# One core, hybrid decoder layer in split f32r products: h's tiles become operands of the output products in place, the last gate reads hL first, the early gate is finished at once, conv tiles are turned later

## The chip, the cores and the metric

One NeuronCore of a Trainium2 chip runs the whole kernel in one launch. The metric is the device time of one execution in microseconds (us); the kernel before took 1667.37 us as the median of three runs (1662.56 to 1667.37). The engines are TensorE (PE, its weight loads are listed apart as PEld), VectorE (DVE), ScalarE (ACT), GpSimd (POOL) and SyncE (SP), which here only issues DMAs.

## The reference

One layer of a decoder trunk over 1024 tokens of width 1024 (S = D = 1024), float32. All branches read the same normalised input, through one big projection:

```python
h = rms_norm(x, norm_g)
proj = h @ w_in                      # 9616 columns
sb_cols, ssd_cols, rw_cols, gate_cols = _split(proj, [2048, 2320, 2176, 3072])
y_sb  = stick_breaking_attention(q, k, v) * silu(sb_gate)      # 8 heads x 64
y_ssd = rms_norm(ssd_mixer(xbc, dt_raw, ...) * silu(z), ssd_norm_g)   # conv of 4 taps, 16 heads, chunks of 128
y_rw  = rwkv7_mixer(rw_cols, ...) * silu(rw_gate)              # 8 heads x 64
g_sb, g_ssd, g_rw = split(sigmoid(gate_cols))                  # 3 x 1024
merged = g_sb*(y_sb @ w_out_sb) + g_ssd*(y_ssd @ w_out_ssd) + g_rw*(y_rw @ w_out_rw)
out = rms_norm(x + merged @ w_o, final_g)
```

## The kernel before, in words

**Split products.** Every large product is made of three f32r matmuls: an operand v is kept as hi (v rounded to f32r) and lo (the rest), and hi·Hi + hi·Lo + lo·Hi go into one PSUM bank. h itself, turned so that its 1024 features lie on partitions, is kept on chip as hH and hL, each 128 x 8 x 1024 (k = 0..7 is the block of features). A weight block of 128 columns comes as `wraw` (one buffer, 512 KB from memory, L193), is cast by ACT into `whi` (L194) and subtracted by DVE into `wlo` (L195), two buffers each; the function is `wload`.

**One projection** (`proj`, L229 to L243) makes 128 columns of the big product: for each half th of the tokens (512) a PSUM bank `pj` (two of them) collects 8 x 3 matmuls of 128x512, a step being the three of one k. So a projection is 16 steps, 48 matmuls. When a half is full, `use` empties it: for the RWKV columns `shift_mix` (ACT L257, DVE L258, a one-column copy `lst` L261, and L264), for the merge gates ACT's sigmoid into `sgt` (L283) and a store to `sgd` in memory, for the conv columns ACT L736, three DVE additions L738 and three small ones L745, then ACT's Silu over the whole tile (L746).

**What sets the order.** TensorE's instructions are written in the order they run. A planner (`Driver`) makes that order: it counts a model time T.t from the matmuls issued, keeps a list `small` of chains (the mixers' small products; a chain may wait a given model time, or for a condition) and issues their next piece when it is due; else it issues one step of the projection at hand (`drv.cur`, `step_big`): first those that the stage needs (`big`), then the 24 merge gates (`spare`), which nothing needs before the output products. Projections are thus the filler between the small products. The planner's numbers fix only the order; the other engines' orders are found by the framework's scheduler from the dependencies, and each engine runs its own list in order.

**Stages.** Start: x is loaded, its rows normalised (`stat`, L297 to L301), turned and split into hH and hL (L309, L310) while two projections already run: `first` (the low-rank RWKV columns, tile `lo`) and `early`, the first merge gate. Their last four steps each alternate, then `drv.cur = first` and `early`, whose second half is still undone, goes back to the front of the gates (L345 to L349): from there it holds one `pj` bank and one `whi`/`wlo` pair until a gate is wanted as filler.
Then RWKV (`rwkv`, 4 units). Then the SSD branch: conv columns c0 to c9; the step sizes dt and the decays da by a chain of small DVE work (to L820), 16 steps of filler (L821), three small products of da with triangle matrices li, ls and on, whose exponentials EX are made on ACT (L824 to L829, all in bank `pma`, of which there are two buffers); then the chunk scan: the conv tiles are turned to token order (`to_tok`, L752) when the tile's conv is done and, for the first group, 2.5 of model time later; then 2 groups x 8 chunks, in which `first(c)` makes the masked decays Mt (L912, L918) and `second(c)` uses them. Then z's gate, a norm (L996) with stores to `yssd`, and 18 steps of filler before the attention's pools take the SSD's space.
Then attention in 4 head pairs: projections Q, K, V, gT of the pair, and 8 rows of 128 queries each (L1097 to L1133): scores, two sigmoids on ACT (be, kp), a mask on POOL, a scan on DVE (L1103), transposes and the product with v. When the projections and gates are all issued, the output products become the filler: `outs` has the RWKV output (`yr`, read back from memory, 4 blocks of k) and then the SSD output (`yssd`, 8 blocks); after the rows come the attention's output and the last product with w_o.

**The output's operands.** `ysplit` loads a block of y (`yt`, four buffers), casts it to yH (L1149, ACT) and subtracts to yL (L1150, DVE). yH and yL have pools of their own (oyA, oyB), which take the space of hH and hL after `hp_ctx.close()`; `reuse_waits="tile"` makes each new tile wait for the tiles whose space it takes. `outp` makes the products, multiplies with the stored merge gate `sg` (L1174 or the lines after it) and stores or adds up `mo`.

Of the kernel before, what the change touches and what calls it, by code (L numbers as in the profile page):

```python
# [8 lines left out]
F32 = mybir.dt.float32  # L9
F32R = mybir.dt.float32r  # L10
# [5 lines left out]
P = 128  # L16
S = 1024
D = 1024
# [120 lines left out]
def body_(tc, A, out):  # L139
# [14 lines left out]
    def pm(tag="a", hold=0.0):  # L154
        drv.bank(tag, hold)
        return psm.tile([P, HB], F32, name="pm" + tag)
# [20 lines left out]
                src = src.rearrange("o (c p) -> (o c) p", p=P)  # L177
            nc.sync.dma_start(out=prow[PO[n]:PO[n] + k, :], in_=src)

    hp_ctx = ctx.enter_context(ExitStack())  # L180
    hp_ = hp_ctx.enter_context(tc.tile_pool(name="hp_", bufs=1, side="right"))
    hH = hp_.tile([P, KT, S], F32R, name="hH")
    hL = hp_.tile([P, KT, S], F32R, name="hL")
    w_in = A["w_in"][0]
# [46 lines left out]
    def proj(c0, use):  # L231

        hi, lo = ahead.pop(c0, None) or wload(w_in[:, c0:c0 + P])
        for th in range(2):
            sl = slice(th * HB, (th + 1) * HB)
            ps = psp.tile([P, HB], F32, name="pj")
            for k in range(KT):
                T.matmul(ps, lhsT=hi[:, k, :], rhs=hH[:, k, sl], start=(k == 0), stop=False)
                T.matmul(ps, lhsT=hi[:, k, :], rhs=hL[:, k, sl], start=False, stop=False)
                T.matmul(ps, lhsT=lo[:, k, :], rhs=hH[:, k, sl], start=False, stop=(k == KT - 1))  # L240
                if k == KT - 1:
                    use(th, ps)
                yield  # L243

    loc = ctx.enter_context(ExitStack())
    lstp = loc.enter_context(tc.tile_pool(name="lstp", bufs=2, side="right"))
    lop = loc.enter_context(tc.tile_pool(name="lop", bufs=1, side="right"))
# [32 lines left out]
    def gate(b, m):  # L280
        def use(th, ps):
            o = gt.tile([P, HB], F32, name="sgt")
            ACT.activation(out=o, in_=ps, func=AF.Sigmoid)  # L283
            nc.sync.dma_start(out=sgd[b, m * P:(m + 1) * P, th * HB:(th + 1) * HB], in_=o)

        return proj(C_GATE + b * D + m * P, use)


    gates = [gate(b, m) for b in (2, 1, 0) for m in range(8)]
# [21 lines left out]

    for t in range(4):
        stat(t)
    pss = [pm("bcbca"[k]) for k in range(5)]
    for i in range(4):
        if i == 3:
# [25 lines left out]
        elif k > 3:  # L342
            next(first)
    x0c.close()
    for _ in range(4):  # L345
        next(first)
        next(early)
    drv.cur = first
    gates.insert(0, early)  # L349


    def rwkv():
# [349 lines left out]
    def ssd():  # L702
# [22 lines left out]
        cT = cc.tile([P, S], F32, name="cT")  # L725
        bt = cc.tile([P, NT, P], F32, name="bt")

        done = set()

        def conv(c, dst):  # L730
            w = lambda k: par("conv_w", k * 10 + c)
            kept = []

            def use(th, ps):
                o = dst[:, th * HB:(th + 1) * HB]
                ACT.activation(out=o, in_=ps, func=AF.Identity, scale=w(3), bias=par("conv_b", c))  # L736
                for d in range(1, 4):
                    stt(out=o[:, d:], in0=ps[:, 0:HB - d], scalar=w(3 - d), in1=o[:, d:], op0=MUL, op1=ADD)  # L738
                if th == 0:
                    lst = wk.tile([P, 3], F32, name="lst")  # L740
                    V.tensor_copy(out=lst, in_=ps[:, HB - 3:HB])
                    kept.append(lst)
                else:
                    for d in range(1, 4):
                        stt(out=o[:, 0:d], in0=kept[0][:, 3 - d:3], scalar=w(3 - d), in1=o[:, 0:d], op0=MUL, op1=ADD)  # L745
                    ACT.activation(out=dst, in_=dst, func=AF.Silu)  # L746
                    done.add("c%d" % c)

            return proj(C_XBC + c * P, use)

# [67 lines left out]
        dal = d1  # L818
        V.tensor_copy(out=dah, in_=da)
        tt(out=dal, in0=da, in1=dah.bitcast(F32), op=SUB)  # L820
        for _ in range(16):  # L821
            drv.step_big()
        EX = []
        for m in (li, ls, on):  # L824
            ps = pm("a")
            T.matmul(ps[:, :P], lhsT=m, rhs=da.rearrange("p c h -> p (c h)"), start=True, stop=True)
            e = cc.tile([P, NT, 16], F32, name="ex%d" % len(EX))
            ACT.activation(out=e.rearrange("p c h -> p (c h)"), in_=ps[:, :P], func=AF.Exp)
            EX.append(e)  # L829
# [38 lines left out]
        def chunks(g):  # L868
# [2 lines left out]
            gh = slice(8 * g, 8 * g + 8)  # L871
            St = Sts[g]
            if g == 0:
                yield 0.0, lambda: "c8" in done and "c9" in done
                yield 2.5
                yield from to_tok(bT, lambda th, ps: ACT.copy(out=bt[:, 4 * th:4 * th + 4, :], in_=ps))
            xt = cc.tile([P, NT, HB], F32, name="xt")
            for k in range(4):
                yield 0.0, lambda: "c%d" % (4 * g + k) in done
                if g == 0:  # L880
                    yield 2.5
                yield from to_tok(yc[:, 4 * g + k, :],
                                  lambda th, ps: ACT.copy(out=xt[:, 4 * th:4 * th + 4, k * P:(k + 1) * P], in_=ps))
                ts(out=yc[:, 4 * g + k, :], in0=yc[:, 4 * g + k, :], scalar1=dsk[:, 4 * g + k:4 * g + k + 1], scalar2=None, op0=MUL)
# [110 lines left out]
        for c in range(8):  # L995
            stt(out=yc[:, c, :], in0=yc[:, c, :], scalar=par("ssd_norm_g", c), in1=acc, op0=MUL, op1=MUL)  # L996
            nc.sync.dma_start(out=yssd[c * P:(c + 1) * P, :], in_=yc[:, c, :])
        for _ in range(18):
            drv.step_big()
        sc.close()  # L1000

# [136 lines left out]

    otp = {}

    def ysplit(pool, ysrc, k0):
        yH = pool.tile([P, 4, S], F32R, name="yH")
        yL = pool.tile([P, 4, S], F32R, name="yL")
        for th in range(2):
            sl = slice(th * HB, (th + 1) * HB)
            for k in range(4):
                yt = otp["p"].tile([P, HB], F32, name="yt", bufs=4)
                nc.sync.dma_start(out=yt, in_=ysrc[(k0 + k) * P:(k0 + k + 1) * P, sl])
                ACT.copy(out=yH[:, k, sl], in_=yt)  # L1149
                tt(out=yL[:, k, sl], in0=yt, in1=yH[:, k, sl].bitcast(F32), op=SUB)  # L1150
        return yH, yL

    def outp(w, gi, ops, first=False, dst=None):
        for m in range(8):
            mw = 2 // len(ops)
            if m % mw == 0:
                hi, lo = wload(A[w][0][:, m * P:(m + mw) * P])
            mc = slice((m % mw) * P, (m % mw + 1) * P)
            for th in range(2):
                sl = slice(th * HB, (th + 1) * HB)  # L1160
                ps = psp.tile([P, HB], F32, name="pj")
                nk = 4 * len(ops)
                for k in range(nk):
                    yield
                    yH, yL = ops[k // 4]
                    j = k % 4
                    T.matmul(ps, lhsT=hi[:, k, mc], rhs=yH[:, j, sl], start=(k == 0), stop=False)
                    T.matmul(ps, lhsT=hi[:, k, mc], rhs=yL[:, j, sl], start=False, stop=False)
                    T.matmul(ps, lhsT=lo[:, k, mc], rhs=yH[:, j, sl], start=False, stop=(k == nk - 1))
                sg = otp["p"].tile([P, HB], F32, name="sg", bufs=OB)  # L1170
                nc.sync.dma_start(out=sg, in_=sgd[gi, m * P:(m + 1) * P, sl])
                mo = otp["p"].tile([P, HB], F32, name="mo", bufs=OB)
                if first:
                    tt(out=mo, in0=ps, in1=sg, op=MUL)  # L1174
                else:
                    nc.sync.dma_start(out=mo, in_=mg[m * P:(m + 1) * P, sl])
                    tt(out=sg, in0=ps, in1=sg, op=MUL)
                    tt(out=mo, in0=sg, in1=mo, op=ADD)
                if dst is None:
                    nc.sync.dma_start(out=mg[m * P:(m + 1) * P, sl], in_=mo)  # L1180
                else:
                    ACT.copy(out=dst[0][:, m, sl], in_=mo)
                    tt(out=dst[1][:, m, sl], in0=mo, in1=dst[0][:, m, sl].bitcast(F32), op=SUB)
# [48 lines left out]
        for i in range(NT):  # L1232
            drv.chain(row(hp, i, tl))
    drv.run(lambda: not drv.big and not drv.spare and drv.cur is None)
    hp_ctx.close()
    oyc = ExitStack()
    oyA = oyc.enter_context(tc.tile_pool(name="oyA", bufs=1, side="right", reuse_waits="tile"))
    oyB = oyc.enter_context(tc.tile_pool(name="oyB", bufs=1, side="right", reuse_waits="tile"))

    def outs():  # L1240
        yield from outp("w_out_rw", 2, [ysplit(oyA, yr, 0)], first=True)
        yB = ysplit(oyB, yssd, 0)
        yA = ysplit(oyA, yssd, 4)
        yield from outp("w_out_ssd", 1, [yB, yA])

    drv.cur = outs()
    drv.run()
    sbp["ctx"].close()
    oyC = ctx.enter_context(tc.tile_pool(name="oyC", bufs=1, reuse_waits="tile"))
    yC = ysplit(oyC, ys, 0)  # L1250
    drv.run(lambda: drv.cur is None)
    oyc.close()
    mp = ctx.enter_context(tc.tile_pool(name="mp", bufs=1, side="right", reuse_waits="tile"))
    mH = mp.tile([P, KT, S], F32R, name="mH")
    mL = mp.tile([P, KT, S], F32R, name="mL")
    fp = ctx.enter_context(tc.tile_pool(name="fp", bufs=1, reuse_waits="tile"))
    wH, wL = load_wo(fp)
    for _ in outp("w_out_sb", 0, [yC], dst=(mH, mL)):
# [27 lines left out]
```

## Time and profile before

| | |
|---|---|
| runs | 1667.37, 1667.37, 1662.56 us |
| profiled execution | 1665.83 us, of it 1664.1 us span from the first to the last instruction |
| PE busy | 1574.4 us (95%), 8565 instructions |
| DVE busy | 972.0 us (58%) |
| ACT busy | 728.2 us (44%) |
| POOL busy | 211.5 us (13%) |
| mean granted TensorE clock | 0.979 of full speed |
| idle before `pj` products, and what ended it (page, part 5) | 27.4 us before pj<-hH,whi (f L258 9.7); 11.5 before pj<-yH,whi (yH L1149 10.4) |

The page's second part shows PE busy in tenths of 40 slices of 41.6 us: 6, 7, 7 in the first three (to 125 us), then 9s, a 7 and an 8 at slices 18 and 19 (the beginning of SSD), an 8 at slice 26 (the attention's first Q), and 8s at slices 33 and 35, where the output products begin. Matmuls overlap; in a run without pauses one 128x512 starts 0.233 us after another though its own record says 0.40. Where the clock is low the record says 0.63 and the next starts 0.43 us later.

### The profile page before, as it was taken

How to read it: one execution, taken by the hardware profiler on the slowest of the kernel's cores; microseconds unless marked ns; L12 is line 12 of the kernel's file. 1: busy time of each engine (PE TensorE's matmuls, PEld its weight loads, DVE VectorE, ACT ScalarE, POOL GpSimd, SP SyncE). 2: the span in 40 equal slices, each digit the busy share in tenths (PEclk: the TensorE clock that was granted, in tenths of full speed). 3: DMA queues.
4: the chain of work that ended last, by engine and by line, in shares of the span. 5: the costliest groups of instructions: out<-in, count | busy, mean ns of one | idle time of the engine just before them, and what ended most of it. 6: DMA issues, size and time to landing. Idle time of an engine off the chain costs nothing.

```text
span 1664.1 us, 22647 instructions
## 1 busy us (share of the span) xinstructions
PE 1574.4 (95%) x8565; PEld 1270.4 (76%) x8565; DVE 972.0 (58%) x1979; ACT 728.2 (44%) x1210; POOL 211.5 (13%) x321
## 2 busy tenths in 40 slices
PE   6779999999999999978999999899999989899998
PEld 4557888887888788756777777777787767688886
DVE  4237577657667673454987934355656566554622
ACT  6125455446445553433445543245545554421211
POOL 0100000000000000100564620121222120000000
PEclk9989999999999999979999999999999999899999
DMA  4203223221322322201011022411211145886422
GB/s 147 58 26 103 64 60 86 64 52 56 79 56 69 87 68 74 63 26 39 26 32 33 26 64 95 152 43 32 59 32 32 45 142 162 276 279 216 133 101 76
DMA packets 189581, 138.72 MB, mean 83 GB/s; under 512 B 42545, under 2 KB 156320, under 8 KB 189472
## 3 DMA queue, kind: packets, MB, share of 16 engines
q1 hardware_dynamic: 189472, 137.28, 27.7%
q8 instruction: 67, 1.10, 0.3%
q14 instruction: 42, 0.34, 0.1%
HBM read 99.50 MB, written 37.75 MB: 82 GB/s over the span
## 4 chain that ended last, share of the span: by engine, by line
PE 78%; DVE 7%; ACT 4%; issue 2%; DMA 1%; POOL 0%; DVEq 0%; SPq 0%; POOLq 0%; ACTq 0%
PE pj L62 52%; PE pmb L62 9%; PE pma L62 9%; PE pmc L62 5%; PE pmb L66 2%; DVE wlo L195 1%; PE pma L66 1%; DVE kp L1103 1%; DMA yt<-yssd 1%; ACT whi L194 1%; DVE TX L538 1%; DVE TB L540 0%; DVE yc L738 0%; ACT aT L1122 0%; DMA sgd<-sgt 0%
## 5 line engine op out<-in xcount | busy, mean ns | idle before, releaser
L62 PE MATMUL pj<-hH,whi 128*128 128x512 f32 x1200 | 505.7, 421 | 27.4 <-DVE f L258 9.7
L62 PE MATMUL pj<-hL,whi 128*128 128x512 f32 x1200 | 480.1, 400 | 0.3 <-DVE hL L310 0.3
L62 PE MATMUL pj<-hH,wlo 128*128 128x512 f32 x1200 | 479.9, 400 | 0.3 <-DVE wlo L195 0.3
L62 PEld LDWEIGHTS pj<-hH,whi 128*128 128x128 f32 x1200 | 229.9, 192 | 84.2 <-DVE f L258 11.5
L62 PEld LDWEIGHTS pj<-hH,wlo 128*128 128x128 f32 x1200 | 229.1, 191 | 56.0 <-DVE wlo L195 1.0
L62 PEld LDWEIGHTS pj<-hL,whi 128*128 128x128 f32 x1200 | 230.2, 192 | 45.0 <-DVE hL L310 1.3
L195 DVE TENSOR_TENSOR wlo<-wraw,whi 128x1024 fp32r<-128x1024 f32 x91 | 112.2, 1233 | 155.0 <-ACT whi L194 151.5
L194 ACT CAST whi<-wraw 128x1024 fp32r<-128x1024 f32 x91 | 95.5, 1049 | 212.6 <-PE pj L62 201.3
L1103 DVE TENSOR_TENSOR_SCAN kp<-kp,one 128x127 f32<-128x127 f32 (+7 forms) x64 | 87.1, 1362 | 65.5 <-POOL kp L1101 64.9
L62 PE MATMUL pj<-yH,whi 128*128 128x512 f32 x256 | 105.0, 410 | 11.5 <-ACT yH L1149 10.4
L62 PE MATMUL pj<-yL,whi 128*128 128x512 f32 x256 | 103.9, 406 | 2.6 <-DVE yL L1150 2.6
L62 PE MATMUL pj<-yH,wlo 128*128 128x512 f32 x256 | 103.0, 402 | 0.0
L62 PEld LDWEIGHTS pj<-yH,whi 128*128 128x128 f32 x256 | 49.5, 194 | 25.6 <-ACT yH L1149 12.6
L1122 ACT COPY aT<-pmb 128x512 f32<-128x512 f32 (+1 forms) x80 | 41.3, 546 | 58.8 <-PE pmb L66 58.5
L635 DVE TENSOR_SCALAR HI<-pmc,GL 64x64 f32<-64x64 f32 x128 | 32.8, 281 | 53.8 <-PE pmc L62 52.6
L62 PEld LDWEIGHTS pj<-yL,whi 128*128 128x128 f32 x256 | 49.5, 193 | 15.7 <-DVE yL L1150 5.2
L1098 ACT ACTIVATE be<-pma 128x384 f32<-128x384 f32 (+3 forms) x96 | 48.2, 502 | 29.5 <-PE pma L62 29.0
L535 POOL TENSOR_SCALAR TB<-id 32x256 f32<-32x256 f32 x16 | 14.2, 890 | 355.0 <-DMA img<-TB 281.2
L62 PEld LDWEIGHTS pj<-yH,wlo 128*128 128x128 f32 x256 | 49.5, 193 | 11.3
L1101 POOL TENSOR_SCALAR_AFFINE_SELECT be<-be 128x128 f32<-128x128 f32 x64 | 25.9, 405 | 232.8 <-ACT be L1098 232.4
L538 DVE TENSOR_TENSOR TX<-CB,TB 32x15 f32<-32x15 f32 (+7 forms) x240 | 46.3, 193 | 9.5 <-POOL TB L535 2.7
L1105 DVE TENSOR_TENSOR be<-be,kp 128x127 f32<-128x127 f32 (+7 forms) x64 | 49.1, 767 | 3.6
(339 smaller groups left out, 2689.1 us busy)
## 6 DMA issues: line engine op xcount, KB each, us to landing
wraw<-in_w_in_dram SPq DMA_DIRECT2D x75, 512.0 KB, 3.6
sgd<-sgt SPq DMA_DIRECT2D x48, 256.0 KB, 2.0
sg<-sgd SPq DMA_DIRECT2D x48, 256.0 KB, 3.3
mg<-mo SPq DMA_DIRECT2D x32, 256.0 KB, 3.0
mo<-mg SPq DMA_DIRECT2D x32, 256.0 KB, 3.4
xt<-in_x_dram SPq DMA_DIRECT2D x8, 512.0 KB, 4.5
Ta<-img SPq DMA_DIRECT2D x16, 256.0 KB, 2.8
Tb<-img SPq DMA_DIRECT2D x16, 256.0 KB, 3.0
```

Of the source, the lines that this page charges most:

```text
L62: return self.eng.matmul(out, lhsT=lhsT, rhs=rhs, **kw)
L66: return self.eng.transpose(**kw)
L194: ACT.copy(out=hi, in_=raw)
L195: tt(out=lo, in0=raw, in1=hi.bitcast(F32), op=SUB)
L535: G.tensor_scalar(out=TB, in0=id16, scalar1=1.0, scalar2=None, op0=MUL)
L538: tt(out=TX[:, j + 1:16, 0:j + 1], in0=CB[:, j, j + 1:16].unsqueeze(2).broadcast_to(sh), in1=TB[:, j:j + 1, 0:j + 1].broadcast_to(sh), op=MUL)
L635: ts(out=HIs[h][cur[h]][0:64, :], in0=o[hr], scalar1=GL[hr, 4 * g + c, h:h + 1], scalar2=None, op0=MUL)
L1098: ACT.activation(out=be[:, b:b + m], in_=ps[:, :m], func=AF.Sigmoid, scale=0.125)
L1101: G.affine_select(out=t_[:, tsl], in_=t_[:, tsl], pattern=[[-1, P]], compare_op=ALU.is_gt, fill=f_, base=0, channel_multiplier=1)
L1103: V.tensor_tensor_scan(out=kp[:, n - 1:0:-1], data0=kp[:, n - 1:0:-1], data1=one.broadcast_to([P, n - 1]), initial=1.0, op0=MUL, op1=MUL)
L1105: tt(out=be[:, 0:n - 1], in0=be[:, 0:n - 1], in1=kp[:, 1:n], op=MUL)
L1122: ACT.copy(out=aT[:, 0:2 * m, :].rearrange("p x t -> p (x t)"), in_=ps[:, :2 * m * P])
```

## The change

Five edits. (1) The pool of hH and hL stays open; `ysplit` is handed its tiles: the halves k = 0..3 and 4..7 of hL are yH and yL of the RWKV output (A_), those of hH are yH and yL of the first half of the SSD output (B_); both splits are issued before the RWKV output product; A_ is used again for the second half of `yssd`. With two operands the first column block opens both halves of the tokens for k = 0..3 before it goes on to k = 4..7. mH and mL, the operands of the last product, are hH and hL. (2) The very last merge gate (branch 0, block 7) does its hL products first, both halves, then those with hH. (3) `first` and `early` are finished one after the other (`rest`), and the weights of `early` are asked for right after the first four `stat`. (4) A conv tile is turned when its conv is done and T.t is 7.0 further; the three products of da come after 24 steps of filler instead of 16 and each in a bank of its own. (5) 24 steps of filler instead of 18 end the SSD stage.

```diff
-    hp_ctx = ctx.enter_context(ExitStack())
-    hp_ = hp_ctx.enter_context(tc.tile_pool(name="hp_", bufs=1, side="right"))
+    hp_ = ctx.enter_context(tc.tile_pool(name="hp_", bufs=1, side="right"))
...
+    def last(c0, use):
+        hi, lo = wload(w_in[:, c0:c0 + P])
+        pss = [psp.tile([P, HB], F32, name="pj") for _ in range(2)]
+        for part in range(2):
+            for th in range(2):
+                sl = slice(th * HB, (th + 1) * HB)
+                for k in range(KT):
+                    if part == 0:
+                        T.matmul(pss[th], lhsT=hi[:, k, :], rhs=hL[:, k, sl], start=(k == 0), stop=False)
+                    else:
+                        T.matmul(pss[th], lhsT=hi[:, k, :], rhs=hH[:, k, sl], start=False, stop=False)
+                        T.matmul(pss[th], lhsT=lo[:, k, :], rhs=hH[:, k, sl], start=False, stop=(k == KT - 1))
...
-        return proj(C_GATE + b * D + m * P, use)
+        return (last if (b, m) == (0, 7) else proj)(C_GATE + b * D + m * P, use)
...
+    ahead[C_GATE + 2 * D] = wload(w_in[:, C_GATE + 2 * D:C_GATE + 2 * D + P])
...
-    for _ in range(4):
-        next(first)
-        next(early)
-    drv.cur = first
-    gates.insert(0, early)
+    def rest():
+        for g in (first, early):
+            yield from g
+    drv.cur = rest()
...
+        turned = lambda n: n in done and T.t >= at[n] + 7.0
...
-        for _ in range(16):
+        for _ in range(24):
             drv.step_big()
...
-            ps = pm("a")
+            ps = pm("abc"[len(EX)])
...
-                yield 0.0, lambda: "c8" in done and "c9" in done
-                yield 2.5
+                yield 0.0, lambda: turned("c8") and "c9" in done
...
-                yield 0.0, lambda: "c%d" % (4 * g + k) in done
-                if g == 0:
-                    yield 2.5
+                yield 0.0, lambda: turned("c%d" % (4 * g + k))
...
-        for _ in range(18):
+        for _ in range(24):
             drv.step_big()
...
-    def ysplit(pool, ysrc, k0):
-        yH = pool.tile([P, 4, S], F32R, name="yH")
-        yL = pool.tile([P, 4, S], F32R, name="yL")
+    def ysplit(ysrc, k0, yH, yL):
...
+            if m == 0 and len(ops) == 2:
+                ks = [(th, k) for k0 in (0, 4) for th in range(2) for k in range(k0, k0 + 4)]
...
-    hp_ctx.close()
-    oyc = ExitStack()
-    oyA = oyc.enter_context(tc.tile_pool(name="oyA", bufs=1, side="right", reuse_waits="tile"))
-    oyB = oyc.enter_context(tc.tile_pool(name="oyB", bufs=1, side="right", reuse_waits="tile"))
+    A_, B_ = ((t_[:, 0:4, :], t_[:, 4:8, :]) for t_ in (hL, hH))
 
     def outs():
-        yield from outp("w_out_rw", 2, [ysplit(oyA, yr, 0)], first=True)
-        yB = ysplit(oyB, yssd, 0)
-        yA = ysplit(oyA, yssd, 4)
+        yA = ysplit(yr, 0, *A_)
+        yB = ysplit(yssd, 0, *B_)
+        yield from outp("w_out_rw", 2, [yA], first=True)
+        yA = ysplit(yssd, 4, *A_)
         yield from outp("w_out_ssd", 1, [yB, yA])
...
-    mH = mp.tile([P, KT, S], F32R, name="mH")
-    mL = mp.tile([P, KT, S], F32R, name="mL")
+    mH, mL = hH, hL
```

The lists of both programs show where instructions stand. ACT's list at the end of the start, before (`lo` is the low-rank tile, `f_525` the first RWKV projection's, `sq` its squares):

```order
L257 ACTIVATE lo<-pj,om 128x512
L272 ACTIVATE lo<-lo 64x1024
L257 ACTIVATE f_525<-pj,om 128x512
L452 ACTIVATE sq<-f_525,pc 128x512
L194 CAST whi<-wraw 128x1024
L257 ACTIVATE f_525<-pj,om 128x512
```

The same place of the changed program (`f_540` is the same tile under its new number):

```order
L274 ACTIVATE lo<-pj,om 128x512
L289 ACTIVATE lo<-lo 64x1024
L193 CAST whi<-wraw 128x1024
L300 ACTIVATE sgt<-pj 128x512
L274 ACTIVATE f_540<-pj,om 128x512
L471 ACTIVATE sq<-f_540,pc 128x512
```

The gate's second half, `sgt`, is now emptied ahead of the first RWKV tile, and with it the weights of the next projection are cast one place earlier; before, that `sgt` stood 25 entries behind the tanh on `lo`, after the unit's four tiles.

PE's list at the three products of da (`d_6059`), before; the rows ahead of and behind the piece are projection steps:

```order
L62 MATMUL pj<-hH,wlo 128x512
L62 MATMUL pma<-d_6059,li 128x128
L62 MATMUL pma<-d_6059,ls 128x128
L62 MATMUL pma<-d_6059,on 128x128
L62 MATMUL pj<-hH,whi 128x512
```

And of the changed program, 24 entries further down its list:

```order
L62 MATMUL pj<-hH,wlo 128x512
L62 MATMUL pma<-d_6059,li 128x128
L62 MATMUL pmb<-d_6059,ls 128x128
L62 MATMUL pmc<-d_6059,on 128x128
L62 MATMUL pj<-hH,whi 128x512
```

24 matmuls of projections (eight steps) have moved ahead of the three, and each has its own bank.

ACT's list of the changed program at the beginning of the output products (`gT` is the last head pair's gate; be, kp and aT belong to the attention's rows; `yt` under the first hH cast is `yssd`):

```order
L1085 ACTIVATE gT<-pj 128x512
L1140 COPY aT<-pmb 128x512
L1165 CAST hH<-yt 128x512 x4
L1116 ACTIVATE be<-pma 128x128
L1117 ACTIVATE kp<-pma 128x128
L1116 ACTIVATE be<-pma 128x128
L1117 ACTIVATE kp<-pma 128x128
L1165 CAST hH<-yt 128x512
```

Before, behind the same `gT` came aT, be and kp without a cast between them, two halves of a merge gate (`sgt`), and the first casts (of yr, into yH) only 21 entries later. In the changed program the casts of yr into hL stand ahead of this `gT`, and those of yssd into hH directly behind it, in front of be and kp.

## Rows read from the trace of the kernel before

**Rows 1.** The page, part 1: busy us, share of the span, instructions.
```profile
PE 1574.4 (95%) x8565; PEld 1270.4 (76%) x8565; DVE 972.0 (58%) x1979; ACT 728.2 (44%) x1210; POOL 211.5 (13%) x321
```

**Rows 2.** Waits of PE: engine, line <- waited for: us in total, times, longest.
```profile
PE pj L62 <- ACT yH L1149: 10.4, 4, 4.3
...
PE pma L66 <- ACT yc L746: 10.1, 4, 3.6
PE pj L62 <- DVE f L258: 9.7, 4, 2.8
PE pj L62 <- DVE lst L261: 6.8, 4, 1.7
PE pma L62 <- ACT kp L1099: 6.1, 6, 1.4
PE pj L62 <- DVE Qs L1040: 4.4, 1, 4.4
...
PE pj L62 <- ACT whi L194: 3.9, 1, 3.9
...
PE pj L62 <- DVE yL L1150: 2.6, 2, 1.4
```

**Rows 3.** Stretches: length, busy (x) per engine, granted PEclk, DMA share, GB/s.
```profile
52.00:100.00 48.00, 37.21 (x133) 28.27 (x132) 6.46 (x12) 6.67 (x9) 0.00 (x0) 0.87 0.12 32
100.00:660.00 560.00, 548.86 (x3379) 461.04 (x3379) 365.35 (x1133) 284.91 (x467) 15.33 (x28) 0.99 0.26 69
...
800.00:950.00 150.00, 149.91 (x845) 116.88 (x842) 132.00 (x180) 81.05 (x101) 87.27 (x65) 1.00 0.11 32
...
1390.00:1440.00 50.00, 41.39 (x207) 30.73 (x205) 28.89 (x39) 21.34 (x36) 0.59 (x2) 0.87 0.70 223
```

**Rows 4.** Timeline of PE: start, us of one, instruction, [idle before <- releaser].
```profile
50.42 0.50 PE L62 MATMUL pj<-hH,whi 128*128 128x512 f32 x1 [2.53 <-DVE lo L258]
...
51.39 0.63 PE L62 MATMUL pj<-hH,whi 128*128 128x512 f32 x1
51.82 0.63 PE L62 MATMUL pj<-hL,whi 128*128 128x512 f32 x1
...
55.10 0.40 PE L62 MATMUL pj<-hL,whi 128*128 128x512 f32 x1
55.33 0.40 PE L62 MATMUL pj<-hH,wlo 128*128 128x512 f32 x1
...
118.71 0.63 PE L62 MATMUL pj<-hH,whi 128*128 128x512 f32 x1
```

**Rows 5.** Timeline of ACT in the start and about the first RWKV tile.
```profile
21.25 1.07 ACT L297 ACTIVATE sq<-xt 128x1024 f32<-128x1024 f32 x1
...
22.29 1.05 ACT L194 CAST whi<-wraw 128x1024 fp32r<-128x1024 f32 x1
...
57.87 0.69 ACT L257 ACTIVATE f<-pj,om 128x512 f32<-128x512 f32 x1 [6.22 <-PE pj L62]
```

**Rows 6.** Timeline of PE at the products of da.
```profile
714.89 0.77 PE L62 MATMUL pma<-d,li 128*128 128x128 f32 x2 [4.30 <-DVE cT L745]
...
719.04 0.77 PE L62 MATMUL pma<-d,on 128*128 128x128 f32 x2 [2.96 <-ACT ex L828]
```

**Rows 7.** Timeline of DVE: the step of da's chain that makes da.
```profile
714.46 0.28 DVE L816 TENSOR_TENSOR d<-dt,hv 128x128 f32<-128x128 f32 x1
```

**Rows 8.** Timeline of PE and of DVE in the last chunk.
```profile
961.95 0.39 PE L62 MATMUL pj<-hH,whi 128*128 128x512 f32 x1
```
```profile
963.27 1.30 DVE L918 TENSOR_TENSOR Mt<-Mt,cb 128x512 f32<-128x512 f32 x2 [1.02 <-ACT Mt L912]
```

**Rows 9.** Timeline of ACT: the first Q cast of the attention.
```profile
1051.77 1.06 ACT L1039 CAST Qs<-pj 64x512 fp32r<-64x512 f32 x2 [0.78 <-DMA sgd<-sgt]
```

**Rows 10.** Timeline of ACT: casts of yr.
```profile
1350.90 1.32 ACT L1149 CAST yH<-yt 128x512 fp32r<-128x512 f32 x2 [4.04 <-DMA yt<-yr]
1353.89 0.62 ACT L1149 CAST yH<-yt 128x512 fp32r<-128x512 f32 x1 [1.66 <-DMA yt<-yr]
```

More of the change, by code (lines that the diff above doesn't have):

```diff
@@ L243, in proj @@
                 yield
+    def last(c0, use):
[10 more added lines that the diff above has]
+                        T.matmul(pss[th], lhsT=lo[:, k, :], rhs=hH[:, k, sl], start=False, stop=(k == KT - 1))
+                    if k == KT - 1 and part:
+                        use(th, pss[th])
+                    if part or k % 2:
+                        yield
     loc = ctx.enter_context(ExitStack())
@@ L726, in ssd @@
         bt = cc.tile([P, NT, P], F32, name="bt")
-        done = set()
+        done, at = set(), {}
+        turned = lambda n: n in done and T.t >= at[n] + 7.0
         def conv(c, dst):
@@ L747, in use @@
                     done.add("c%d" % c)
+                    at["c%d" % c] = T.t
             return proj(C_XBC + c * P, use)
@@ L1158, in outp @@
             mc = slice((m % mw) * P, (m % mw + 1) * P)
-            for th in range(2):
-                sl = slice(th * HB, (th + 1) * HB)
[L1161 to L1169, printed above, removed]
+            nk = 4 * len(ops)
+            pss = [psp.tile([P, HB], F32, name="pj")]
+            ks = [(th, k) for th in range(2) for k in range(nk)]
+            if m == 0 and len(ops) == 2:
+                ks = [(th, k) for k0 in (0, 4) for th in range(2) for k in range(k0, k0 + 4)]
+            for th, k in ks:
+                yield
+                if th == len(pss):
+                    pss.append(psp.tile([P, HB], F32, name="pj"))
+                ps = pss[th]
+                sl = slice(th * HB, (th + 1) * HB)
+                yH, yL = ops[k // 4]
+                j = k % 4
+                T.matmul(ps, lhsT=hi[:, k, mc], rhs=yH[:, j, sl], start=(k == 0), stop=False)
+                T.matmul(ps, lhsT=hi[:, k, mc], rhs=yL[:, j, sl], start=False, stop=False)
+                T.matmul(ps, lhsT=lo[:, k, mc], rhs=yH[:, j, sl], start=False, stop=(k == nk - 1))
+                if k < nk - 1:
+                    continue
                 sg = otp["p"].tile([P, HB], F32, name="sg", bufs=OB)
@@ L1249, in body_ @@
     oyC = ctx.enter_context(tc.tile_pool(name="oyC", bufs=1, reuse_waits="tile"))
-    yC = ysplit(oyC, ys, 0)
+    yC = ysplit(ys, 0, oyC.tile([P, 4, S], F32R, name="yH"), oyC.tile([P, 4, S], F32R, name="yL"))
     drv.run(lambda: drv.cur is None)
-    oyc.close()
-    mp = ctx.enter_context(tc.tile_pool(name="mp", bufs=1, side="right", reuse_waits="tile"))
-    mH = mp.tile([P, KT, S], F32R, name="mH")
-    mL = mp.tile([P, KT, S], F32R, name="mL")
+    mH, mL = hH, hL
     fp = ctx.enter_context(tc.tile_pool(name="fp", bufs=1, reuse_waits="tile"))
```

## Prediction

> **What bounds the kernel now.** I read the page's busy shares first: PE works 1574.4 us, the next engine (DVE) 972.0 [rows 1]. In a span of 1664.1 us, TensorE can therefore gain only from its pauses (1664.1 − 1574.4 = 89.7 us) and from stretches at a low clock. Both engines issue the same products after the change, so nothing is removed from the 1574.4 us but what the clock adds to it. The list of PE's waits tells who ends the pauses [rows 2]; the stretches tell where they lie [rows 3]. They are not spread out: between 100 and 660 us PE works 548.9 of 560 us and between 800 and 950 us 149.9 of 150, while 52 to 100 and 1390 to 1440 us have 37.2 of 48 and 41.4 of 50, both with a granted clock of 0.87. The edits work at these places, so I go through them by place, and then look at what each edit moves away.
>
> The clock has to be priced beside the pause. After the pause of 2.53 us that ends at 50.42, records of 128x512 read 0.63 us and start 0.43 us apart (51.39, 51.82); from 54.4 on they read 0.40 and start 0.23 apart (55.10, 55.33) [rows 4]. These are the clock's two levels, 1.2 and 2.4 GHz. Each product at the low level costs 0.427 − 0.233 = 0.194 us extra. I counted PE's 128x512 records of 0.63 us or more: 39 from 51.39 to 118.71 [rows 4], and of the same kind 18 between 700 and 790, 7 behind 1054.55 and 29 between 1340 and 1440.
>
> **A. The start, 47.9 to 128 us.** Before, the unfinished early gate holds one `pj` bank and one weight pair, so each half of a projection waits for the eviction of the half before it: f L258 9.7 us in 4 waits, lst L261 6.8 in 4, and 2.5 on lo [rows 2, 4], 19.0 us in all. Finished at once, the gate gives bank and weights back. Its remaining 24 products (24 x 0.233 = 5.6 us) come just where PE waited for lo, whose eviction is then covered, and its own eviction (one sigmoid) stands in ACT's list ahead of the first RWKV tile's, which waits idle there for 6.2 us [rows 5]. So all nine waits go, and with them 39 x 0.194 = 7.6 us of low clock: 26.6. Against it stands what the pauses had hidden: the first unit's preparation (the small products of lo, the squares, the tables) now meets PE earlier. Its work on ACT and DVE is light there (6.7 and 6.5 us busy of 48 [rows 3]), so I put new waits at 1.5, between 0 and one wait of each former pair (2.8 + 1.7 = 4.5). A = 25.1 (22 to 26.6).
>
> The weights asked for ahead don't help: in ACT's list the cast still stands behind the two squares of x, and before it runs at 22.29 directly after them [rows 5]. The pause of 3.9 us on whi [rows 2] stays; I count 0.
>
> **B. The beginning of SSD, 705 to 790 us.** Before, PE comes to da's first product with nothing else allowed, and stands 4.30 us; da's chain ended at 714.74 [rows 6, 7], though the row names cT, a conv addition that ends at the same time. The third product waits 2.96 us more for the bank that the first's exponential empties. Four turns of conv tiles wait 10.1 us for the Silu [rows 2]. Together 17.4 us. Eight more steps (8 x 3 x 0.233 = 5.6 us) cover the 4.30; a bank each removes the 2.96. For the turns the delay in model time is raised from 2.5 to 7; the longest wait was 3.6, so 4.5 more is enough by a little, if model and chip time run alike over it (over the steps between, 0.233 us per product, they nearly do). With the low clock's 18 x 0.194 = 3.5, the gain is 20.9. The price: the steps used here and at SSD's end are missing in the scan. By PE's order no projection step now lies between `first` and `second` of the last chunk; before, they ran from 961.95 on [rows 8]. Mt is ready at 963.27 + 1.30 = 964.57, and of the 2.6 us from 961.95 the small products that are left cover a fraction: I take 2.3, between 0 and 4 (the wait and 7 products at low clock). B = 18.6 (14 to 21).
>
> **C. The first Q, 1050 to 1054.6 us.** PE waits 4.4 us for Qs [rows 2], whose cast could not begin before 1051.77 [rows 9]: Qs lies in the space of the conv tiles, and these are still being stored. Six more steps at SSD's end (6 x 3 x 0.233 = 4.2 us) begin one more gate, which is finished first (48 x 0.233 = 11.2 us in all). Q's first half, which ended at about 1050, then ends 4 to 11 us later against the stores, behind the 1051.77 at which the space was free. Gain 4.4 + 7 x 0.194 = 5.8. What is late next is nothing that I can see: the cast itself, 1.06 us, is hidden by the second half.
>
> **D. The output products, 1342 to 1435 us.** PE waits 10.4 us on yH and 2.6 on yL [rows 2]: operands are loaded, cast and subtracted when PE already needs them, because their space was not free until h's last reader was done, and the first column block of the SSD product needs all eight blocks at once. In place, a cast into hL block k and half th waits only for that block's last reader. The special last gate is not that reader: by PE's order it has run long before, as more gates are used up earlier, and the last to read hL is the projection gT of the last head pair. So that edit does nothing for the wait; but yr's casts still stand ahead of gT's in ACT's list and run beside its second half (5.6 us). The first half of yssd is split beside the RWKV product (8 blocks x 2 halves x 4 k, 64 steps, 45 us), and the second half comes behind 8 steps of the first block. That removes 13.0 us and the low clock of 29 x 0.194 = 5.6: 18.6. Some of it comes back: the casts into hH wait for loads into four `yt` buffers, and aT, be and kp of the attention's rows stand behind them on ACT. Nothing in the trace shows just that; the nearest rows are the casts that waited 4.04 and 1.66 us for loads of yr [rows 10]. Bounds: 0 (PE has other products ready) and 5.7 (both as waits of PE); I take 4, by the longer of the two rows, since be and kp begin a chain over POOL and DVE that nothing shortens. D = 14.6 (13 to 18.6, less if the wait is paid again with low clock).
>
> For this term a rule bears on the change: the Trainium skill, page "PSUM — Partial Sum Buffer", section "Engine vs sequencer instructions", says that ScalarE's queue is strictly first in, first out. The trace agrees: before the casts at 1350.90 and 1353.89 ACT was idle for 4.04 and 1.66 us, and nothing from behind them ran. By the rule up to 5.7 us of the gain is returned; if ACT could pass over a waiting cast, none would be.
>
> **Sum.** 25.1 + 18.6 + 5.8 + 14.6 = 64.1. The rest is small waits moved about: attention rows lose a gate of filler and gain output steps; I take off 2, for one or two more waits of the kind on kp (6.1 in 6, 1.4 at most [rows 2]), bounds 0 and 8 (six of the longest anew). The profiled execution took 1665.8 us, 1.6 less than the median shown; 1665.8 − 62.1 = 1603.7, and I say **1604**.
>
> **Rivals.**
> *Part comes back (1617 to 1631).* Output stage and start are held by the chain of load, cast and subtract rather than by the order: D gives nothing (1604 + 14.6 = 1619), or A's preparation becomes the bound and A gives half (1604 + 12.6 = 1617), or both (1631). For it: DMA share is 0.70 in 1390 to 1440 already [rows 3], and ACT waits for loads there. Against: PE's waits in A are all on evictions of a single bank.
> *The parts that I count as nothing work, and no new wait comes (about 1593).* The early weights save the 3.9 us, and the 1.5, 2.3, 4 and 2 us of new waits are absent, the most of it: 1604 − 11. For it: none of these waits is in the trace. Against: ACT's order is unchanged at the start.
> *Slower (1671).* The filler spent early is missing all through the scan: each chunk without a projection between `first` and `second` pays the 2.6 us to Mt and about 8 products at low clock after it (1.6), 4.2 us. The 62.1 us are used up at 15 of the 16 chunks; all 16 give 1604 + 15 x 4.2 = 1667 (one is in the sum), and with DVE, which is busy 132 of 150 us there [rows 3], late by 0.3 us in each as well, 1671. It decides from the 15th chunk; by the order it is one. That the change has no effect at all needs the same sum to come out near 62.
>
> **How the numbers follow.** The forecast has 0.62, with a range of its own of 1594 to 1615; part back 0.25; more than counted 0.08; slower 0.02; no difference 0.03 (0.3%, 5 us, is about what a measurement of this kernel can tell from none). Reaching into both sides: the bounds of the terms sum to 22 + 14 + 5.8 + 13 − 8 = 47 (1619) and 26.6 + 21 + 5.8 + 18.6 = 72 (1594); with A and D cut it is 1631, and with the early weights at work 1590. The range is 1588 to 1630. Faster 0.95, same 0.03, slower 0.02.
>
> **What would show it.** In the profile after: A is right if from 48 to 128 us PE has no pauses on f, lst and lo and PEclk is near 1.0; B if the rows of da's products and of the conv turns carry no idle time, and there is one new wait of 2 to 3 us on Mt or a row beside it, some 45 us earlier than the 962 of before; C if Q's first half follows with no gap; D if PE's list of waits has no yH and yL (now hH, hL) over 2 us, and new waits, if any, on aT, be or kp with ACT waiting for `yt`. The pause ended by whi at the start should be as long as before. It is wrong if the scan (before, 800 to 950) shows PE idle in many chunks, if PEclk stays near 0.87 where SSD or the output products begin, or if gaps as long as before stand at the same places with other names.

## The result, and the profile after

The changed kernel takes 1596.97 us (median of four runs, 1596.66 to 1597.15), the kernel before 1666.06 (1662.56 to 1667.37): 0.9588 of it, 95% interval 0.9572 to 0.9605. The forecast was 1604, in a range of 1588 to 1630.

The page's first two parts after, to be held against [rows 1]:

```profile
span 1595.4 us, 22632 instructions
...
PE 1550.2 (97%) x8565; PEld 1255.6 (79%) x8565; DVE 967.4 (61%) x1979; ACT 726.8 (46%) x1210; POOL 210.7 (13%) x321
...
PE   6999999999999999999999999999999999999998
```

The span is 68.7 us shorter. PE's busy time fell by 24.2 us for the same 8565 instructions: that is for the most part the clock, whose mean rose from 0.979 to 0.996. The other 44.5 us are pauses. The stretches after (start and end, length, busy us per engine, clock, DMA share, GB/s) stand against [rows 3]; the first is the start from 48 us on, then RWKV, the beginning of SSD, the scan, and the output products beside and behind the attention's last rows:

```profile
48.00:110.00 62.00, 62.00 (x270) 48.15 (x269) 25.75 (x51) 25.05 (x33) 1.29 (x4) 1.00 0.28 77
110.00:640.00 530.00, 518.46 (x3245) 437.01 (x3244) 349.17 (x1104) 268.12 (x446) 15.79 (x27) 1.00 0.26 69
700.00:800.00 100.00, 98.86 (x522) 77.95 (x521) 75.78 (x128) 49.70 (x65) 28.23 (x24) 1.00 0.14 37
755.00:905.00 150.00, 149.80 (x838) 116.76 (x837) 129.62 (x178) 80.64 (x100) 85.59 (x65) 1.00 0.13 36
1286.00:1345.00 59.00, 58.55 (x370) 46.98 (x369) 47.37 (x62) 33.44 (x73) 11.38 (x30) 1.00 0.57 181
1340.00:1390.00 50.00, 48.36 (x265) 38.50 (x264) 31.17 (x43) 22.20 (x37) 1.18 (x4) 1.00 0.71 228
```

And PE's waits after (us in total, times, longest), to be held against [rows 2]:

```profile
PE pmb L66 <- DVE xn L318: 10.1, 1, 10.1
PE pma L62 <- ACT kp L1117: 5.3, 5, 1.4
PE pmb L62 <- ACT tmp L616: 4.7, 2, 3.0
PE pj L62 <- ACT whi L193: 3.9, 1, 3.9
PE pj L62 <- DVE sg L1200: 2.9, 4, 1.2
PE pmb L62 <- DVE tmp L622: 1.9, 5, 0.6
PE pmc L62 <- ACT Z L643: 1.7, 3, 0.8
PE pj L62 <- DVE mo L1197: 1.4, 2, 1.1
PE pma L62 <- DVE Mt L936: 1.0, 1, 1.0
PE pma L66 <- ACT yc L766: 0.9, 1, 0.9
```

All waits that were forecast to go are gone or down to one of 0.9: f, lst, lo, cT, ex, Qs and both names of the output operands. The wait on whi is what it was. New are the waits on tmp and Z in the RWKV units (PE idle 11.5 us between 128 and 640 us, before 5.4) and on sg at the end.

### The profile page after: what moved, and what is told of

Same layout as the page of the kernel before. It is cut to its first block, busy times and chain, and to the rows that moved or that the text cites. A ratio compares the mean times of both kernels' runs of the same rounds, so it can differ in the third digit from the quotient of the medians.

```text
span 1595.4 us, 22632 instructions
## 1 busy us (share of the span) xinstructions
PE 1550.2 (97%) x8565; PEld 1255.6 (79%) x8565; DVE 967.4 (61%) x1979; ACT 726.8 (46%) x1210; POOL 210.7 (13%) x321
## 4 chain that ended last, share of the span: by engine, by line
PE 78%; DVE 8%; ACT 5%; issue 4%; DMA 3%; POOL 0%; SPq 0%; DVEq 0%; POOLq 0%; ACTq 0%
PE pj L62 52%; PE pma L62 9%; PE pmb L62 9%; PE pmc L62 4%; PE pmb L66 2%; DVE wlo L194 1%; PE pma L66 1%; DVE kp L1121 1%; DMA yt<-in_w_o_dram 1%; DVE TX L557 1%; DVE TB L559 1%; ACT whi L193 1%; DMA mg<-mo 1%; DMA sg<-sgd 0%; ACT kp L1117 0%
## 5 line engine op out<-in xcount | busy, mean ns | idle before, releaser
L62 PE MATMUL pj<-hL,whi 128*128 128x512 f32 x1456 | 554.8, 397 | 1.8 <-DVE mo L1197 1.4
L62 PE MATMUL pj<-hH,whi 128*128 128x512 f32 x1328 | 540.0, 414 | 6.9 <-ACT whi L193 3.9
L62 PE MATMUL pj<-hH,wlo 128*128 128x512 f32 x1264 | 501.0, 396 | 0.0
L62 PEld LDWEIGHTS pj<-hL,whi 128*128 128x128 f32 x1456 | 273.8, 189 | 57.4 <-DVE mo L1197 2.3
L62 PE MATMUL pj<-hL,wlo 128*128 128x512 f32 x128 | 50.7, 396 | 0.0
L559 DVE TENSOR_TENSOR TB<-TB,TX 32x15 f32<-32x15 f32 (+7 forms) x240 | 46.4, 193 | 6.0
L1117 ACT ACTIVATE kp<-pma 128x384 f32<-128x384 f32 (+3 forms) x96 | 48.4, 505 | 1.5 <-DVE be L1123 1.5
L925 POOL TENSOR_TENSOR DL<-li,d 128x512 fp32r<-128x512 f32 x32 | 45.6, 1435 | 25.1 <-DVE d L841 18.7
L62 PEld LDWEIGHTS pmc<-HI,Z 128*128 128x128 f32 x256 | 37.3, 190 | 7.9 <-ACT Z L643 2.8
L62 PE MATMUL pma<-Ks,Qs 128*128 128x384 f32 (+3 forms) x96 | 36.9, 390 | 5.3 <-ACT kp L1117 5.3
```

Source lines behind the costliest of these rows:

```text
L62: return self.eng.matmul(out, lhsT=lhsT, rhs=rhs, **kw)
L559: tt(out=TB[:, j + 1:16, 0:j + 1], in0=TB[:, j + 1:16, 0:j + 1], in1=TX[:, j + 1:16, 0:j + 1], op=SUB)
L925: G.tensor_tensor(out=DL, in0=lb, in1=dal[:, c, h0:h0 + 4].unsqueeze(2).broadcast_to([P, 4, P]), op=MUL)
L1117: ACT.activation(out=kp[:, b:b + m], in_=ps[:, :m], func=AF.Sigmoid, scale=-0.125)
```

## Experiments

Each part of the change was undone alone, then parts together; every kernel ran beside the kernel before. Times are medians of four runs. "Over" is the distance from 1596.97. A kernel's ratio to the kernel before carries an interval of about 0.002 to either side, so an "over" of 3 us is at the edge of what can be told from none.

**The early gate left half done again.**

```diff
-    drv.cur = rest()
+    for _ in range(4):
+        next(first)
+        next(early)
+    drv.cur = first
+    gates.insert(0, early)
```

> The changed kernel with one part undone: the early gate is left half done again (the last four steps of first and early alternate, then the gate goes to the front of the gates). Theory (each place has its own edit): the nine pauses on f, lst and lo come back with their low clock, 27.7 us of pauses and clock between 48 and 128 us; the 7 us of new waits and clock that the RWKV units show in the changed kernel (tmp L616, Z, ZLe) go, since PE reaches them later: 1597 + 27.7 - 7.0 = 1618. Rival 1 (the RWKV units' new waits have another cause, such as the gate that is no longer there as filler in a later unit, and stay): 1625. Rival 2 (the start is bound elsewhere and the gain of that stretch came from the weights asked for ahead): under 1605.

1613.83 us (1611.55 to 1615.09), 16.9 over. The waits of PE that came back are those of before, to a tenth:

```profile
PE pj L62 <- DVE f L275: 9.7, 4, 2.8
PE pj L62 <- DVE lst L278: 6.8, 4, 1.7
...
PE pj L62 <- DVE lo L275: 2.5, 1, 2.5
PE pmb L62 <- ACT tmp L615: 1.7, 1, 1.7
```

The RWKV units' idle time is back at 5.3 us, so their new waits belong to this edit. But the clock is not back. In the stretch of the nine pauses the kernel before had

```profile
48.00:100.00 52.00, 38.79 (x136) 29.57 (x137) 8.87 (x19) 8.35 (x12) 0.12 (x1) 0.87 0.18 49
```

and this one, with the same pauses,

```profile
48.00:100.00 52.00, 37.14 (x148) 27.84 (x146) 10.40 (x24) 10.87 (x14) 1.00 (x3) 0.97 0.18 51
```

at 0.97 instead of 0.87; between 48 and 120 us 13 products of 128x512 stand at the low level (0.63 us) instead of 39. Two kernels further down, edit 1 alone and 24 steps alone, have the start of the kernel before with its nine pauses too; both show 0.90 in this stretch, and 33 and 32 slow products. Whether this kernel's small loss is its own or that of the one execution that was profiled is not shown. That execution (1611.55 us, the shortest of the four) has a span 14.4 us longer than the changed kernel's (1609.8 against 1595.4); 19.0 us of pauses less 6.2 of new waits make 12.8 of them.

**Products of da and turns as before.** (16 steps, bank a, 2.5 of model time in the first group)

```diff
-        for _ in range(24):
+        for _ in range(16):
...
-            ps = pm("abc"[len(EX)])
+            ps = pm("a")
...
-                yield 0.0, lambda: turned("c%d" % (4 * g + k))
+                yield 0.0, lambda: "c%d" % (4 * g + k) in done
+                if g == 0:
+                    yield 2.5
```

> The changed kernel with one part undone: 16 steps of filler before the products of da, all three in bank a, conv tiles turned 2.5 of model time after their conv in the first group and at once in the second. Theory: the waits at da's products and at the turns come back (before: 17.3 us of pauses and 5.3 of clock; the changed kernel has 0.9 and 1.7), so 1597 + 20 = 1617. Rival (the steps spent early cost something in the scan, which is now given back, 2 us or more, in the last chunk): 1615 or less, with the 0.99 us wait on Mt gone.

1622.31 us (1620.28 to 1623.32), 25.3 over: yc 10.1, cT 4.3 and ex 3.0 are back as before, and PE's busy time is 7.1 us longer. The pauses are about those of the theory (17.9 us by the spans and busy times); that busy time is why it came out 5 us above it. In the last chunk the 0.99 on Mt gives way to the 1.23 on yo that the kernel before had there: the rival fell, the steps spent early cost the scan nothing on balance.

**18 steps at SSD's end.** (`range(24)` to `range(18)`)

> The changed kernel with one part undone: 18 steps of filler instead of 24 at the end of the SSD stage. Theory: the wait of 4.4 us for Q's space and its low clock come back, 1597 + 6 = 1603, and at the output products nothing changes, whichever projection reads hL last. Rival (the six steps also freed h earlier for the output products, since one more gate is used up before the last projection): casts of yr wait again, 10 us or more of pauses on hL: 1613 or more.

1603.47 us (1602.28 to 1603.80), 6.5 over. The wait on Qs is back with 4.5 us. At the output products nothing comes back on balance (1.3 us on hL and 1.3 on aT, against 2.5 less on sg and 1.4 less on mo), although the last merge gate now ends at 1302 us instead of 1143, behind the last head pair's gT.

**Pools of their own for yH and yL.** (`hp_` closed, oyA, oyB and mp opened, the SSD splits behind the RWKV output product; the order of k as changed)

> The changed kernel with one part undone: yH and yL in pools of their own again, opened after hp_ is closed, the second and third splits issued after the RWKV output product, mH and mL tiles of their own; the order of k in the first SSD block stays as changed, and all other edits stay. Theory (place decides): 10 to 13 us of pauses on yH and yL and 5 to 9 of clock come back: 1597 + 18 = 1615. Rival (the gates finish earlier through the other edits, and this is what freed the output products): under 1603.

1599.84 us (1596.32 to 1602.91), 2.9 over, and its range takes in that of the changed kernel: the theory fell, the rival held. With **all of edit 1 undone**, the order of k too:

> The changed kernel with all of edit 1 undone: pools of their own, splits issued late, and the first SSD block in the plain order of k. Theory 1 (either the place or the order of k frees the output products): the waits on yH come back in the first SSD block, which needs all eight blocks of yssd at once, 4 to 8 us with some clock: 1604 to 1612. Theory 2 (the other edits alone free them, since the RWKV output product now ends before the attention's last rows and the SSD splits are issued ahead of the attention's own): 1603 or less.

1599.95 us (1599.66 to 1600.23), 3.0 over; the interval of its ratio (0.9584 to 0.9622) overlaps with that of the changed kernel. The trace has 2.0 us on yH and 0.5 on yL back, both at the first products with yr. So edit 1 is worth 3 us at most here. **Edit 1 alone** on the kernel before (the main lines that come in; those that they replace are left out):

```diff
+    A_, B_ = ((t_[:, 0:4, :], t_[:, 4:8, :]) for t_ in (hL, hH))
...
+        yA = ysplit(yr, 0, *A_)
+        yB = ysplit(yssd, 0, *B_)
+        yield from outp("w_out_rw", 2, [yA], first=True)
+        yA = ysplit(yssd, 4, *A_)
```

> The kernel before with edit 1 alone (operands in the tiles of h, the two first splits issued ahead of the RWKV output product, the order of k in the first SSD block, mH and mL in place). Theory 1 (edit 1 is enough by itself; the run without pools only showed that the other edits are enough too): the 14 us of pauses and some 5 to 9 us of clock between 1340 and 1440 us go, 1665 - 18 = 1647. Theory 2 (the output products were freed by the gates that are finished earlier, edit 1 does little): 1660 or more, with pauses of 8 us or more on hL and hH.

1653.35 us (1652.05 to 1653.90), 0.9923 of before (0.9906 to 0.9940), 11.4 less: between the two theories, and much more than 3. The waits on the operands are down to 1.2 us (hL), but PE stands 3.7 us behind a `mo` and then makes 6 products at the low level; where this wait comes from is shown below, with the plain last gate. What an edit is worth depends on which others are there. **24 steps alone** on the kernel before:

```diff
-        for _ in range(18):
+        for _ in range(24):
             drv.step_big()
         sc.close()
```

> The kernel before with 24 steps instead of 18 at SSD's end, nothing else. Theory 1 (as in the run beside it): the wait for Q goes, and most of the waits of the output products too, 1665 - 6.5 - 16 = 1643 (1639 to 1648). Theory 2: only the wait for Q goes, 1659.

1644.23 us (1641.69 to 1645.57), 0.9879 (0.9859 to 0.9898), 21.2 less, for an edit that by its place is worth 6.5. And **both undone** in the changed kernel, edit 1 and the 24 steps:

> The changed kernel with all of edit 1 undone and 18 steps instead of 24 at SSD's end (edits 2, 3 and 4 stay). Theory 1 (the output products are freed by either of two edits: the operands' place, or the gate that the six steps use up, after which the RWKV output product ends before the attention's rows): now both are gone, so the waits on yH and yL and their clock are back, 14 to 23 us, with the 6.5 us for Q: 1597 + 6.5 + 18 = 1621 (1615 to 1627). Theory 2 (the edits at the start and at SSD's beginning free them): 1597 + 6.5 + 3 = 1606.

1620.09 us (1618.37 to 1620.67), 23.1 over, where the single ones give 3.0 and 6.5. In the changed kernel either of the two frees the output products, and only without both the waits are back (PE's waits of this kernel):

```profile
PE pj L62 <- ACT yH L1168: 8.7, 4, 4.4
...
PE pj L62 <- DVE yL L1169: 2.0, 3, 1.3
```

ACT's timeline shows how. With both undone, the RWKV output product (64 steps) outlasts the attention's rows; when these end, the attention's own output `ys` is split first, and the SSD blocks, which PE needs earlier, come behind it:

```profile
1370.73 1.88 ACT L1168 CAST yH<-yt 128x512 fp32r<-128x512 f32 x3 [5.31 <-DMA yt<-ys]
...
1376.79 0.62 ACT L1168 CAST yH<-yt 128x512 fp32r<-128x512 f32 x1 [0.23 <-DMA yt<-yssd]
```

With 24 steps the last gate is done at 1143 us instead of beside the rows, the RWKV output product starts one gate earlier against them and ends within them, and the first half of yssd is split some 75 us before ys (the run with edit 1 undone):

```profile
1299.14 1.28 ACT L1168 CAST yH<-yt 128x512 fp32r<-128x512 f32 x2 [0.46 <-DMA yt<-yssd]
...
1376.89 1.25 ACT L1168 CAST yH<-yt 128x512 fp32r<-128x512 f32 x2 [2.60 <-DMA yt<-ys]
```

Edit 1 gets the same order by issuing that split ahead of the product.

**No special last gate, no early weights.** (`proj` for every gate, the `ahead` line out)

> The changed kernel without the special last gate and without the early weights asked for ahead. As predicted neither does anything: 1597, within 1.5. Rival: the pause on whi at the start grows beyond 3.9, or casts into hL wait: 1600 or more.

1597.87 us (1596.61 to 1600.16): as expected, neither does anything. **18 steps and a plain last gate**, where that gate is the last to read hL:

> The changed kernel with 18 steps at SSD's end and a plain last gate; there the gate is the last projection, and its hL products are the last readers of hL. Compare with the run of 18 steps that has the special gate, 1603.5. If reading hL first is worth what it is meant for, casts of yr into hL wait longer here and PE with them: 1606 or more. If not: within 1.5 of 1603.5.

1608.54 us (1607.23 to 1609.50), 5.1 more than 18 steps with the special gate. So the special gate is worth this much where it comes last, but not by the wait that was expected: PE's waits on hL are 1.2 us here and 1.3 there. The casts into hL stretch to 1297 us instead of 1293, so the last load of yssd is issued at 1307 instead of 1299, and four of the subtractions of yssd (L1166) come to stand on DVE between the first product's `mo` and the second's. Until that second `mo` is made, PE waits for its bank:

```profile
1306.92 0.67 DVE L1197 TENSOR_TENSOR mo<-pj,sg 128x512 f32<-128x512 f32 x1
...
1309.55 1.37 DVE L1166 TENSOR_TENSOR hH<-yt,hH 128x512 fp32r<-128x512 f32 x2
...
1313.42 0.66 DVE L1166 TENSOR_TENSOR hH<-yt,hH 128x512 fp32r<-128x512 f32 x1
...
1314.73 1.28 DVE L1197 TENSOR_TENSOR mo<-pj,sg 128x512 f32<-128x512 f32 x2
...
1315.47 1.18 PE L62 MATMUL pj<-hL,whi 128*128 128x512 f32 x2 [3.23 <-DVE mo L1197]
```

With the special gate the subtractions are done at 1306.8, by the first `mo`, and PE does not wait there. The run with edit 1 alone, which has the plain gate last too, shows the same order: four subtractions between the two `mo`, and PE idle 3.65 us. Where the gate comes last, edit 1 needs edit 2.

**Two tries to do better.** A longer model delay in the RWKV chain (`LAT = 2.0` to `2.6`):

> The changed kernel with the planner's delay behind an ACT or DVE step of the RWKV chain raised from 2.0 to 2.6 (LAT). If the new waits in the RWKV units (tmp 4.7 and 1.9, Z 1.7, ZLe 0.8 us) are PE coming too early for the real latency: up to 6 us less, 1591. If the units are bound by the chain's own length, the wait only moves: 1597 or more.

1621.75 us (1618.93 to 1623.89), 24.8 over. The waits on tmp and Z fall from 9.1 to 1.3 us, but others on Yq and sq stand in their place (6.6 and 3.9): the RWKV stage, which now ends some 25 us later, idles 11.9 us (128 to 685) where it idled 11.5 (128 to 660). The wait moved, as the second theory says. And the units take two more gates as filler, so that the scan, which must leave four, has none left: 15.5 us of idle time between 800 and 960 us, where it was 1.0.

```profile
PE pmc L66 <- DVE Yq L671: 6.6, 2, 4.4
PE pmb L62 <- DVE DH L924: 6.2, 2, 3.8
...
PE pma L62 <- DVE Mt L936: 4.2, 1, 4.2
...
PE pmc L62 <- DVE St L958: 3.5, 1, 3.5
```

The two exponentials of an RWKV preparation put together by priority:

> The changed kernel with the two exponentials of an RWKV preparation given a high priority, so that they stand together on ACT and no table is loaded between them. If the wait of 3.04 us on tmp at 267 us comes from the table loads ahead of the copy in ACT's list (two of 1.28 us for the square root between the exponentials), 1.3 to 3 us go: 1594 to 1596. If not, 1597 and the same wait.

1596.53 us (1595.70 to 1599.64), the same. The priority did not bring them together: the square root and its table still stand between, and the copy PE waits for behind them.

```profile
264.81 0.63 ACT L463 ACTIVATE E<-sg 128x512 f32<-128x512 f32 x1
265.46 1.28 ACT L478 ACT_TABLE_LOAD   x1
266.76 0.18 ACT L478 ACTIVATE inv<-pma 128x8 f32<-128x8 f32 x1
266.95 1.28 ACT L464 ACT_TABLE_LOAD   x1
268.25 0.63 ACT L464 ACTIVATE sg<-sg 128x512 f32<-128x512 f32 x1
268.78 0.57 ACT L617 COPY tmp<-pmb 128x512 f32<-128x512 f32 x1
```

The run with the early gate left half done has the other order: the exponentials stand together with one load behind them, and PE does not wait there.

```profile
282.81 0.63 ACT L460 ACTIVATE E<-sg 128x512 f32<-128x512 f32 x1
283.47 0.63 ACT L462 ACTIVATE sg<-sg 128x512 f32<-128x512 f32 x1
284.12 1.28 ACT L476 ACT_TABLE_LOAD   x1
...
285.49 0.58 ACT L615 COPY tmp<-pmb 128x512 f32<-128x512 f32 x1
```

So the 3.04 us go with this order in ACT's list; what the loads alone make of it, no run shows, since none changed only the order. No version beats the changed kernel.

## Why the prediction was right, and where it was not

**A (25.1).** The nine pauses and their cause were right. The step that was mis-sized is the new waits, put at 1.5 with 4.5 as the bound: the units idle 6.2 us more. I had looked at the first unit alone and bounded them by one wait of each kind at the start; they fall in the later units, and half of them (3.04) is the place where two table loads stand ahead of ACT's copy. The clock's 7.6 us are what the trace of before shows, but the same pauses left fewer slow products in other runs (33, 32 and 13 for 39); undone, the edit costs 16.9.

**The early weights and the last gate (0 each).** Right, shown by the run without both (with 24 steps no run took out one alone). That the gate had run long before the output products was read from PE's order; the run with 18 steps shows that it would have mattered there.

**B (18.6).** The pauses were right (17.4, now 0.9 at one turn). The price of 2.3 for the last chunk was wrong: the wait on Mt is 0.99, and it replaces one of 1.23 on yo at the same place. Undone, the part costs 25.3, 4.4 above the sum's unreduced 20.9; 7.1 of it is longer busy time of PE, where the sum had 3.5 for the clock and counted products of 128x512 alone.

**C (5.8).** Right; 6.5 measured, with the wait of 4.5 back when the steps are undone.

**D (14.6).** Here the step that failed is the cause. I gave the waits on yH and yL to the space that was not free until h's last reader was done; more than half of them were due to order, the SSD splits behind those of ys. Of the 13.0 us 5.5 stand at the first products with yr, behind the last gate, and 7.5 at those with yssd. The trace of before had it, in PE's timeline and in ACT's at the end of the attention's rows:

```profile
1345.36 0.79 PE L62 MATMUL pj<-yH,whi 128*128 128x512 f32 x1 [2.87 <-ACT yH L1149]
...
1423.09 0.76 PE L62 MATMUL pj<-yH,whi 128*128 128x512 f32 x1 [2.37 <-ACT yH L1149]
...
1434.56 0.79 PE L62 MATMUL pj<-yH,whi 128*128 128x512 f32 x1 [4.26 <-ACT yH L1149]
```

```profile
1417.21 1.91 ACT L1149 CAST yH<-yt 128x512 fp32r<-128x512 f32 x3 [6.33 <-DMA yt<-ys]
...
1429.60 1.26 ACT L1149 CAST yH<-yt 128x512 fp32r<-128x512 f32 x2 [2.19 <-DMA yt<-yssd]
```

The casts of yssd waited for loads, behind those of ys, not for the space of h, and PE's longest wait (4.3, to 1434.6) was on them. I had seen that the extra gate moves the output products and counted it only at Q. That the size came out near is luck: the cause was wrong for half of the waits, but both edits that free the products were made. The idle time of this work fell from 14.1 us (1340 to 1440) to 2.1 (1280 to 1380 after) and the 29 slow products to none, 17.6 by the prediction's price for one; three new waits on sg behind it take 2.4 back. The price of 4 for casts in front of be and kp was not paid: ACT waited for loads of yssd 2.9 us in three, and PE for none of that. The rule of the Trainium skill on ScalarE's strict order (page "PSUM — Partial Sum Buffer", section "Engine vs sequencer instructions") agrees with the trace, since ACT did stand idle before those casts. PE had other products all the while, and the lower bound of 0 was the right end.

**Sum.** 69.1 against 62.1. Undone one at a time, edits 4, 3, 5 and 1 cost 25.3, 16.9, 6.5 and 3.0, together 51.7, which leaves 17.4. Of these, 13.6 are the output products', which either of two edits frees: undone together edits 5 and 1 cost 23.1, one at a time 6.5 and 3.0 (23.1 − 9.5 = 13.6). The other 3.8 no run separates. The term of 2 for small waits was about right (kp from 6.1 to 5.3, sg 2.9 new).

**Rivals.** "Part comes back" did not happen. "The parts that I count as nothing work" came near in time (1593) but not in cause: the early weights saved nothing, and of the new waits only those put at 2.3 and 4 were absent, while those of the RWKV units were four times as large as I had put them. "Slower" has its mechanism in the run with the longer delay: filler that is spent early is missing in the scan, at 24.8 us; the change itself stays clear of it.

## What to carry to other kernels

Where a planner fills gaps from a finite stock of free work, every edit that shifts the stock acts at a far place too: follow the stock through all stages (here, at which time the last gate ends) before giving a wait to the edit that stands beside it. A wait for an operand has two possible causes, its space and its place in the queue that makes it; look at what ran ahead of it in that queue. And when parts of a change are undone alone and the costs don't add up to the whole, undo pairs.

## What was not expected of the hardware

Four kernels have the same nine pauses at the start (18.7 to 19.1 us in all, 1.26 to 2.82 each). In their profiled executions these left 39, 33, 32 and 13 products at the lower clock level, with granted clocks of 0.86, 0.88, 0.88 and 0.95 between 48 and 120 us. In the third and the fourth (24 steps alone, and the early gate left half done) the first five pauses end within 0.2 us of each other; behind the fifth the one runs at the low level, the other does not:

```profile
85.20 0.80 PE L62 MATMUL pj<-hH,whi 128*128 128x512 f32 x1 [2.82 <-DVE f L258]
85.80 0.63 PE L62 MATMUL pj<-hL,whi 128*128 128x512 f32 x1
```

```profile
85.04 0.50 PE L62 MATMUL pj<-hH,whi 128*128 128x512 f32 x1 [2.82 <-DVE f L275]
```

What decides it is not shown. A term for the clock read from one trace is then good to a few us per stretch only.
